# Seven block products in two more pieces of each feed-forward's first 512 gate units, and activation sums begun earlier

## The chip, the cores and the metric

The kernel runs on one core of one Trainium2 chip. The time is device microseconds (us) of one execution. The kernel before takes 2220.28 us (median of three runs, 2219.53 to 2221.06).

## The reference

A two-layer bidirectional encoder trunk in float32 on 256 tokens of width 2048. Layer 0 mixes tokens with a bidirectional mLSTM and an RG-LRU; layer 1 with 16-head dilated attention. Each layer ends in a SwiGLU feed-forward, and it is this part that the change touches:

```python
def rmsnorm(x, g):
    xf = x.astype(jnp.float32)
    y = xf * lax.rsqrt(jnp.mean(jnp.square(xf), axis=-1, keepdims=True) + RMS_EPS)
    return (y * g.astype(jnp.float32)).astype(x.dtype)

def swiglu(h, w1, w3, w2):
    return (jax.nn.silu(h @ w1) * (h @ w3)) @ w2
...
        x = x + dilated_attention(h, o_w_qkv[o], o_w_o[o]).astype(x.dtype)   # or the layer-0 mixer
        h = rmsnorm(x, f_norm[l])
        x = x + swiglu(h, f_w1[l], f_w3[l], f_w2[l]).astype(x.dtype)
```

Here `w1` (gate) and `w3` are 2048 x 5632 and `w2` is 5632 x 2048, so the hidden units form 11 blocks of 512 units, numbered 0 to 10 below.

## The kernel before

**Precision.** A float32 product is made of three products of rounded halves. Activations and weights are each split into a high part (rounded to the fp32r format) and a low part (what is left). For each weight tile ScalarE casts the high half (`wh`, L228) and VectorE subtracts to get the low half (`wl`, L229). TensorE then adds high x high, high x low and low x high in PSUM (L300 to L302 in `narrow`).

**Pieces and steps.** A weight piece is 512 input rows by 512 output columns, one transfer of 1 MB by SyncE's queue into one of three buffers (`raw`). A piece is two steps, each of 256 input rows. A plain step is 12 matmuls of 512 columns: two row blocks of 128, two token halves, three products. The list `steps` is written out in program order; `emit_step` emits one step's matmuls, and before them the split of the step three places ahead (`AHEAD`), so VectorE and ScalarE see the work of step s+3 before TensorE's step s. After each step `run_tasks` lets every waiting generator (an evacuation, a sum, an attention head) go on to its next `yield`; at most three background tasks run at once. So a task with k yields is spread over k steps, unless `until(flag)` finds its flag missing at emission: then tasks are run on at once, without steps between them.

**Seven products.** Some gate pieces (`w1`, blocks 1 to 10, pieces g = 1, 2, 3 of four) use a 2 x 2 block scheme with seven block products in place of eight (`seven_products`, L305 to L338): 21 matmuls of 256 columns a step. It needs sums of weight blocks, made once per piece (`weight_sums`, L197 to L211: four VectorE subtractions L202 to L205, then three ScalarE casts L209 and three VectorE remainders L210), and sums of activation blocks (`sf`), made once per feed-forward by the task `act_sums`: for each of six pairs of row blocks (kb = 4, 6 of piece 1; 8, 10 of piece 2; 12, 14 of piece 3) five VectorE instructions (L1067, L1071, L1072, L1074, L1075), a ScalarE cast (L1077) and a VectorE remainder (L1079), with five yields. Block 0 uses plain steps alone. The sums need `xT`, the normalised transposed activations, whose quarter g is written by the evacuation of column chunk g of the output projection ahead of the feed-forward (`norm_evac`: L414 adds the residual, ScalarE squares, TensorE transposes into `nT`, L440 and L441 write `xT`).

**Around a block.** For each block the pieces alternate, w1 piece 0, w3 piece 0, w1 piece 1, and so on: 16 steps. The gate's sum lies in two PSUM buffers `acc`, with seven products in two more (`ext`) out of the same pool of four; w3's sum lies in the pool of two (`mx`). `up1` evacuates the gate: with `ext` by one ScalarE copy (L1003) and six VectorE additions (L1004 to L1009), then the Silu (L1011); `up3` multiplies it in (L1027), which frees the two `mx` buffers for the next block's w3, and transposes to `hT` (L1040, L1041). After three blocks come the matching steps of w2.

**Buffers.** Large tiles come from eight slots of 2112 elements a partition (`slot`).

Of the kernel before, what the change touches and what calls it, by code (L numbers as in the profile page):

```python
# [9 lines left out]
F32 = mybir.dt.float32  # L10
F32R = mybir.dt.float32r
# [6 lines left out]
P = 128  # L18
# [11 lines left out]
SEVEN = (1, 2, 3)  # L30
# [38 lines left out]
def trunk_kernel(ctx: ExitStack, tc: tile.TileContext, a, out):  # L69
# [14 lines left out]
    mxp = ctx.enter_context(tc.tile_pool(name="mxp", bufs=2, space=PSUM))  # L84
    ctx.enter_context(tc.manual_schedule())

    def slot(shape, dt=F32, name="s8"):
        t = s8p.tile([P, SLOT], dt, tag="s8", name=name)
        n = int(np.prod(shape))
        v = t[:, :n]  # L90
        if len(shape) == 1:
            return v
        pat = {2: "p (a b) -> p a b", 3: "p (a b c) -> p a b c", 4: "p (a b c d) -> p a b c d"}[len(shape)]
        return v.rearrange(pat, **dict(zip("abcd"[1:], shape[1:])))
# [6 lines left out]
    def ev(name="ev"):  # L101
        return evp.tile([P, CW], F32, tag="ev", name=name)
# [50 lines left out]
    steps = []  # L153
# [17 lines left out]
    def wload(src, n):  # L171
        def load(t):
            if n < 4:
                m = 2 if n else 1
                for k in range(0, 4, m):
                    load_xT(4 * n + k, m)
                    SP.dma_start(t[:, k:k + m, :], src[:, k:k + m, :])
                return
            SP.dma_start(t, src)

        return load
# [57 lines left out]
    def add_unit(src, ch, kb0, first, last, act, seven=None):  # L239

        items.append(wload(src, len(items)))
        it = len(items) - 1
        for h in range(2):
            steps.append({
                "item": it, "half": h, "last_half": h == 1, "ch": ch, "kb": kb0 + 2 * h, "act": act,
                "first": first and h == 0, "last": last and h == 1, "wide": False, "before": None, "seven": seven,
            })
# [21 lines left out]
    urgent, queue, active = [], [], []  # L269
# [190 lines left out]
    def act_norm(gains):  # L460
        def act(kb):
            until(f"xT{gains}_{kb // 4}")
            return act_x(kb)

        return act
# [523 lines left out]
    def ffn(l, gains, nxt):  # L989
        st = {}  # L990
        act = act_norm(gains)

        def up1(c):
            def gen(ch):
                while f"rstd{gains}" not in flags:
                    yield
                es = [ev("up") for t in range(2)]
                if ch.ext:
                    (c0, c1), (e0, e1) = ch.acc, ch.ext
                    l_, r_ = slice(0, 256), slice(256, CW)  # L1000
                    x0, x1 = es
                    u2 = ev("u2")[:, l_]
                    A.copy(x0, e0)  # L1003
                    V.tensor_tensor(u2, e1[:, l_], x0[:, l_], op=ALU.add)  # L1004
                    V.tensor_tensor(x1[:, l_], e1[:, r_], u2, op=ALU.add)
                    V.tensor_tensor(x1[:, r_], x1[:, l_], x0[:, r_], op=ALU.add)
                    V.tensor_tensor(x0[:, r_], x0[:, r_], u2, op=ALU.add)
                    V.tensor_tensor(x0, c0, x0, op=ALU.add)
                    V.tensor_tensor(x1, c1, x1, op=ALU.add)  # L1009
                for t in range(2):  # L1010
                    A.activation(es[t], es[t] if ch.ext else ch.acc[t], AF.Silu, scale=cur["rstd"][:, t:t + 1])  # L1011
                ch.acc = ch.ext = None
                st["e", c] = es
                flags.add(f"up{l}_{c}")
                yield

            return gen

        def up3(c):


            def gen(ch):
                while f"up{l}_{c}" not in flags:
                    yield
                es = st.pop(("e", c))
                for t in range(2):
                    V.scalar_tensor_tensor(  # L1027
                        es[t], ch.acc[t], cur["rstd"][:, t:t + 1], es[t], op0=ALU.mult, op1=ALU.mult
                    )
                ch.acc = None  # L1030
                yield
                yield from lag()
                h = st["h", c] = slot((4, 2, S), F32R, name="hT")
                for p in range(2):
                    ps = tp("hTp")
                    for k in range(2):
                        f0 = (2 * p + k) * P
                        for t in range(2):
                            transpose(ps[:, k, t * P:(t + 1) * P], es[t][:, f0:f0 + P])
                    A.copy(h[:, 2 * p:2 * p + 2, 0, :], ps)  # L1040
                    V.tensor_tensor(  # L1041
                        h[:, 2 * p:2 * p + 2, 1, :], ps, h[:, 2 * p:2 * p + 2, 0, :].bitcast(F32), op=ALU.subtract
                    )
                    for k in range(2):
                        flags.add(f"h{l}_{4 * c + 2 * p + k}")
                    yield

            return gen

        def act_h(kb):  # L1050
            until(f"h{l}_{kb}")
            return st["h", kb // 4][:, kb % 4]

        sf = {}

        def act_sums():

            for g in SEVEN:
                while f"xT{gains}_{g}" not in flags:
                    yield  # L1060
                two = slot((2, 4, 2, P), F32R, "sf")
                for j, kb in enumerate((4 * g, 4 * g + 2)):
                    f = two[:, j]
                    v = ev("sa")
                    x = xT[:, kb:kb + 2].bitcast(F32)
                    vv = v.rearrange("p (j t) -> p j t", j=2)
                    V.tensor_tensor(vv, x[:, :, 0, :], x[:, :, 1, :], op=ALU.add)  # L1067
                    a11, a21, a12, a22 = (vv[:, j, t * P:(t + 1) * P] for j in range(2) for t in range(2))
                    w = ev("sb").rearrange("p (k t) -> p k t", k=4)
                    yield  # L1070
                    V.tensor_tensor(w[:, 0], a21, a22, op=ALU.add)  # L1071
                    V.tensor_tensor(w[:, 2], a11, a21, op=ALU.subtract)  # L1072
                    yield
                    V.tensor_tensor(w[:, 1], w[:, 0], a11, op=ALU.subtract)  # L1074
                    V.tensor_tensor(w[:, 3], a12, w[:, 1], op=ALU.subtract)  # L1075
                    yield
                    A.copy(f[:, :, 0, :], w)  # L1077
                    yield
                    V.tensor_tensor(f[:, :, 1, :], w, f[:, :, 0, :].bitcast(F32), op=ALU.subtract)  # L1079
                    sf[kb] = f  # L1080
                    flags.add(f"sf{l}_{kb}")
                    yield

        def seven(kb):
            until(f"sf{l}_{kb}")
            return sf[kb]

        at_first = len(steps)
        for hidx, (c0, c1) in enumerate(UPS):
            for c in range(c0, c1):  # L1090
                chs = Chunk(up1(c)), Chunk(up3(c))
                chs[1].small = True
                for g in range(4):
                    add_unit(a["w1"][l, c][g], chs[0], 4 * g, g == 0, g == 3, act,
                             seven if c and g in SEVEN else None)
                    add_unit(a["w3"][l, c][g], chs[1], 4 * g, g == 0, g == 3, act)
            last = hidx == len(UPS) - 1
            if last:
                ssq = const.tile([P, 2, NCD], F32, name=f"ssq{l}")
            chs = []  # L1100
            for n in range(NCD):
                if not last:
                    def evac(ch, n=n):
                        c_ = (n % 2) * CW
                        for t in range(2):
                            dst = xt[n // 2][:, t, c_:c_ + CW]
                            V.tensor_tensor(dst, ch.acc[t], dst, op=ALU.add)
                        ch.acc = None
                        yield
                else:  # L1110
                    evac = norm_evac(n, nxt, ssq, xt, last=nxt < 0)
                chs.append(Chunk(evac))
            for n, kgs in ((0, range(c0, c1 - 1)), (1, range(c0, c1 - 1)), (0, (c1 - 1,)), (1, (c1 - 1,)),
                           (2, range(c0, c1)), (3, range(c0, c1))):
                for kg in kgs:
                    add_unit(a["w2"][l, n][kg], chs[n], 4 * kg, kg == c0, kg == c1 - 1, act_h)
        steps[at_first]["before"] = lambda: queue.append(act_sums())
        return ssq


# [82 lines left out]
    act = act_norm(G_O)  # L1203
# [33 lines left out]
    n = NCD - 1  # L1237
# [104 lines left out]
```

## Time and profile before

| | |
|---|---|
| time, median of three runs | 2220.28 us (2219.53 to 2221.06) |
| the profiled execution's own time | 2219.59 us |
| its span | 2217.8 us |
| TensorE busy | 2195.3 us (99%) |
| VectorE busy | 1588.9 us (72%) |
| ScalarE busy | 1156.3 us (52%) |
| DMA | 417.53 MB, mean 188 GB/s |

The span runs from the first to the last instruction; the execution is 1.8 us longer. PE is TensorE's matmuls, PEld its weight loads, DVE VectorE, ACT ScalarE, POOL GpSimd, SP SyncE. A matmul's shown duration reaches past the start of the next one, so rates are read from the distance of starts. The first feed-forward begins at about 364 us, the second at about 1484 us.

### The profile page before, as it was taken

The page shows a single profiled execution, that of the slowest core. Times are in us where ns is not written, and L with a number is a line of the kernel's source. Part 1 is how long each engine was busy: PE and PEld are TensorE (multiplying, and loading weights), DVE is VectorE, ACT ScalarE, POOL GpSimd, SP SyncE. Part 2 cuts the span into 40 slices and gives each one's busy share as a digit, 9 for nine tenths or more (in the row PEclk, how much of TensorE's full clock was granted, in tenths as well). Part 3 has the DMA queues.
Part 4 walks back from the last instruction along what each step waited for, and adds up shares of the span by engine and source line. Part 5 has one row for each costly group of instructions (what it writes and reads, how often), then busy time and mean ns, then how long its engine had stood idle before and what let it go on. Part 6 is the DMA issues. An engine that isn't in the chain of part 4 may idle for free.

```text
span 2217.8 us, 28894 instructions
## 1 busy us (share of the span) xinstructions
PE 2195.3 (99%) x11492; PEld 1881.5 (85%) x11492; DVE 1588.9 (72%) x2160; ACT 1156.3 (52%) x1555; POOL 22.6 (1%) x37
## 2 busy tenths in 40 slices
PE   9999999999999999999999999999999999999998
PEld 7887888888888888888888888888888888888886
DVE  6877756875787688578666676567867885886686
ACT  6666555544455455445554555455544553554454
POOL 0000000000000000000000000000000000000000
PEclk9999999999999999999999999999999999999999
DMA  7444555555555555555554555455555655555653
GB/s 280 174 143 148 193 201 199 171 190 190 199 181 207 179 201 201 194 197 191 177 191 174 180 185 175 171 182 180 189 190 190 208 190 190 183 203 197 215 192 131
DMA packets 61471, 417.53 MB, mean 188 GB/s; under 512 B 7060, under 2 KB 7956, under 8 KB 12568
## 3 DMA queue, kind: packets, MB, share of 16 engines
q1 hardware_dynamic: 58616, 406.69, 52.9%
q0 software_dynamic: 2288, 8.39, 1.1%
q8 instruction: 90, 1.47, 0.2%
q10 hardware_dynamic: 432, 0.61, 0.1%
q14 instruction: 45, 0.37, 0.0%
HBM read 413.56 MB, written 2.10 MB: 187 GB/s over the span
## 4 chain that ended last, share of the span: by engine, by line
PE 90%; DVE 6%; ACT 2%; issue 1%; DMA 0%; SPq 0%; POOL 0%; POOLq 0%; DVEq 0%; ACTq 0%
PE acc L300 20%; PE acc L301 20%; PE acc L302 20%; PE acc L361 9%; PE acc L362 5%; PE ext L338 2%; PE ext L337 2%; PE ext L336 2%; DVE wl L229 2%; PE acc L338 2%; PE acc L336 2%; PE acc L337 2%; ACT wh L228 1%; PE hTp L146 1%; PE rgp L524 1%
## 5 line engine op out<-in xcount | busy, mean ns | idle before, releaser
L229 DVE TENSOR_TENSOR wl<-raw,wh 128x1024 fp32r<-128x1024 f32 (+1 forms) x770 | 928.7, 1220 | 519.9 <-ACT wh L228 517.1
L228 ACT CAST wh<-raw 128x1024 fp32r<-128x1024 f32 (+1 forms) x770 | 794.0, 1046 | 518.8 <-PE acc L302 376.2
L300 PE MATMUL acc<-wh,xT 128*128 128x512 f32 x1184 | 467.5, 395 | 0.0
L301 PE MATMUL acc<-wl,xT 128*128 128x512 f32 x1184 | 462.9, 391 | 1.0 <-DVE wl L229 1.0
L302 PE MATMUL acc<-wh,xT 128*128 128x512 f32 x1184 | 461.6, 390 | 0.0
L361 PE MATMUL acc<-xT,wh 128*128 128x512 f32 x896 | 321.7, 402 | 0.5 <-ACT v L731 0.5
L300 PE MATMUL acc<-wh,hT 128*128 128x512 f32 x704 | 276.1, 392 | 0.0
L302 PE MATMUL acc<-wh,hT 128*128 128x512 f32 x704 | 274.3, 390 | 0.0
L301 PE MATMUL acc<-wl,hT 128*128 128x512 f32 x704 | 274.1, 389 | 0.1
L302 PEld LDWEIGHTS acc<-wh,xT 128*128 128x128 f32 x1184 | 222.7, 188 | 47.2
L300 PEld LDWEIGHTS acc<-wh,xT 128*128 128x128 f32 x1184 | 223.4, 189 | 45.7 <-issue 1.5
L301 PEld LDWEIGHTS acc<-wl,xT 128*128 128x128 f32 x1184 | 223.1, 188 | 44.9 <-DVE wl L229 2.3
L362 PE MATMUL acc<-xT,wl 128*128 128x256 f32 x896 | 251.2, 280 | 0.2 <-DVE wl L229 0.2
L209 ACT CAST wf<-ws 128x512 fp32r<-128x512 f32 x180 | 111.9, 622 | 201.1 <-DVE ws L202 152.5
L361 PEld LDWEIGHTS acc<-xT,wh 128*128 128x128 f32 x896 | 168.3, 188 | 39.5 <-ACT v L731 0.6
L362 PEld LDWEIGHTS acc<-xT,wl 128*128 128x128 f32 x896 | 169.2, 189 | 1.1 <-DVE wl L229 0.5
L302 PEld LDWEIGHTS acc<-wh,hT 128*128 128x128 f32 x704 | 132.1, 188 | 27.8
L301 PEld LDWEIGHTS acc<-wl,hT 128*128 128x128 f32 x704 | 132.3, 188 | 27.4 <-DVE wl L229 0.5
L300 PEld LDWEIGHTS acc<-wh,hT 128*128 128x128 f32 x704 | 132.2, 188 | 26.8
L210 DVE TENSOR_TENSOR wf<-ws,wf 128x512 fp32r<-128x512 f32 x180 | 113.3, 684 | 0.0
L338 PE MATMUL ext<-wf,sf 128*128 128x256 f32 x240 | 68.7, 286 | 4.6 <-DVE sf L1079 4.6
L336 PE MATMUL ext<-wf,sf 128*128 128x256 f32 x240 | 68.3, 285 | 3.6 <-ACT sf L1077 3.6
(278 smaller groups left out, 2731.8 us busy)
## 6 DMA issues: line engine op xcount, KB each, us to landing
raw<-in_w SPq DMA_DIRECT2D x264, 1024.0 KB, 4.9
raw<-in_w_aqk SPq DMA_DIRECT2D x32, 1024.0 KB, 4.9
raw<-in_w_out SPq DMA_DIRECT2D x16, 1024.0 KB, 4.9
raw<-in_w_av SPq DMA_DIRECT2D x16, 1024.0 KB, 4.9
raw<-in_w_o SPq DMA_DIRECT2D x16, 1024.0 KB, 4.9
raw<-in_w_xr SPq DMA_DIRECT2D x8, 1024.0 KB, 6.8
raw<-in_w_qk SPq DMA_DIRECT2D x8, 1024.0 KB, 4.9
raw<-in_w_og SPq DMA_DIRECT2D x8, 1024.0 KB, 4.8
```

The source lines that it names most:

```text
L209: A.copy(f[:, 0], t)
L210: V.tensor_tensor(f[:, 1], t, f[:, 0].bitcast(F32), op=ALU.subtract)
L228: A.copy(hi[:, k], raw[:, k])
L229: V.tensor_tensor(lo[:, k], raw[:, k], hi[:, k].bitcast(F32), op=ALU.subtract)
L300: PE.matmul(acc, xh, hi[:, j, :], start=f, stop=False)
L301: PE.matmul(acc, xh, lo[:, j, :], start=False, stop=False)
L302: PE.matmul(acc, xl, hi[:, j, :], start=False, stop=e)
L336: PE.matmul(o, xh, wh, start=new, stop=False)
L337: PE.matmul(o, xh, wl, start=False, stop=False)
L338: PE.matmul(o, xl, wh, start=False, stop=end)
L361: PE.matmul(acc, wh[:, j, :], x2.rearrange("p a b -> p (a b)"), start=f, stop=False)
L362: PE.matmul(acc[:, :S], wl[:, j, :], x2[:, 0, :], start=False, stop=e)
```

## The change

Four edits.

1. In block 0 the gate's pieces are taken in the order 0, 3, 1, 2, and the last two of these (pieces 1 and 2) use seven products. w3's pieces keep their order. Blocks 1 to 10 stay as they are.
2. So block 0's evacuation takes the way with `ext`, and each of the two pieces gets its weight sums.
3. The task `act_sums` is put in the queue 12 steps earlier, that is 12 steps before the end of the output projection, in place of at the feed-forward's first step. It still waits for the flag of each quarter of `xT`.
4. The tile of activation sums starts 56 elements (224 bytes) into its slot.

```diff
-    def slot(shape, dt=F32, name="s8"):
+    def slot(shape, dt=F32, name="s8", off=0):
         t = s8p.tile([P, SLOT], dt, tag="s8", name=name)
         n = int(np.prod(shape))
-        v = t[:, :n]
+        v = t[:, off:off + n]
...
-                two = slot((2, 4, 2, P), F32R, "sf")
+                two = slot((2, 4, 2, P), F32R, "sf", off=56)
...
-                for g in range(4):
-                    add_unit(a["w1"][l, c][g], chs[0], 4 * g, g == 0, g == 3, act,
-                             seven if c and g in SEVEN else None)
-                    add_unit(a["w3"][l, c][g], chs[1], 4 * g, g == 0, g == 3, act)
+
+                order, at_seven = (range(4), SEVEN) if c else ((0, 3, 1, 2), (2, 3))
+                for k, g in enumerate(order):
+                    add_unit(a["w1"][l, c][g], chs[0], 4 * g, k == 0, k == 3, act,
+                             seven if k in at_seven else None)
+                    add_unit(a["w3"][l, c][k], chs[1], 4 * k, k == 0, k == 3, act)
...
-        steps[at_first]["before"] = lambda: queue.append(act_sums())
+        steps[at_first - 12]["before"] = lambda: queue.append(act_sums())
```

**Where the instructions now stand, first place.** VectorE at the end of the first output projection. L414 and L441 are the evacuation of its column chunks, L229 the splits of coming steps, L1067 to L1079 the activation sums. Before, from the splits ahead of the last chunk's evacuation on:

```order
L229 TENSOR_TENSOR wl<-raw,wh 128x1024 x5
L414 TENSOR_TENSOR xres<-acc,xres 128x512 x2
L229 TENSOR_TENSOR wl<-raw,wh 128x1024
L441 SCALAR_TENSOR_TENSOR xT<-nT,cpk,xT 128x256 x4
L448 TENSOR_REDUCE rstd_3180<-ssq_o_115 128x2
L449 TENSOR_SCALAR rstd_3180<-rstd_3180 128x2
L1067 TENSOR_TENSOR sa<-xT 128x512
L229 TENSOR_TENSOR wl<-raw,wh 128x1024
L1071 TENSOR_TENSOR sb<-sa 128x128
L1072 TENSOR_TENSOR sb<-sa 128x128
L229 TENSOR_TENSOR wl<-raw,wh 128x1024
L1074 TENSOR_TENSOR sb<-sb,sa 128x128
```

And now, from the evacuation of the second chunk on:

```order
L441 SCALAR_TENSOR_TENSOR xT<-nT,cpk,xT 128x256 x2
L229 TENSOR_TENSOR wl<-raw,wh 128x1024 x2
L1067 TENSOR_TENSOR sa<-xT 128x512
L229 TENSOR_TENSOR wl<-raw,wh 128x1024
L1071 TENSOR_TENSOR sb<-sa 128x128
L1072 TENSOR_TENSOR sb<-sa 128x128
L229 TENSOR_TENSOR wl<-raw,wh 128x1024
L1074 TENSOR_TENSOR sb<-sb,sa 128x128
L1075 TENSOR_TENSOR sb<-sa,sb 128x128
L229 TENSOR_TENSOR wl<-raw,wh 128x1024 x2
L414 TENSOR_TENSOR xres<-acc,xres 128x512 x2
L1079 TENSOR_TENSOR sf<-sb,sf 128x4x128
```

The first pair's sums now stand ahead of the third chunk's evacuation (this L414), where before they stood behind the fourth's.

**Second place.** VectorE where the last pair's sum (the sixth L1079, kb = 14) is written. L202 to L210 are weight sums of a coming gate piece. Before, in block 1, behind that block's third weight sums and ahead of its evacuation (L1004):

```order
L229 TENSOR_TENSOR wl<-raw,wh 128x1024
L1067 TENSOR_TENSOR sa<-xT 128x512
L229 TENSOR_TENSOR wl<-raw,wh 128x1024
L1071 TENSOR_TENSOR sb<-sa 128x128
L1072 TENSOR_TENSOR sb<-sa 128x128
L229 TENSOR_TENSOR wl<-raw,wh 128x1024
L1074 TENSOR_TENSOR sb<-sb,sa 128x128
L1075 TENSOR_TENSOR sb<-sa,sb 128x128
L229 TENSOR_TENSOR wl<-raw,wh 128x1024 x2
L1079 TENSOR_TENSOR sf<-sb,sf 128x4x128
L229 TENSOR_TENSOR wl<-raw,wh 128x1024
L1004 TENSOR_TENSOR u_3884<-ext,up 128x256
```

And now, right behind block 0's evacuation, around the first weight sums of block 1:

```order
L229 TENSOR_TENSOR wl<-raw,wh 128x1024
L1074 TENSOR_TENSOR sb<-sb,sa 128x128
L1075 TENSOR_TENSOR sb<-sa,sb 128x128
L229 TENSOR_TENSOR wl<-raw,wh 128x1024
L1027 SCALAR_TENSOR_TENSOR up<-acc,rstd_3205,up 128x512 x2
L202 TENSOR_TENSOR ws<-raw 128x512
L203 TENSOR_TENSOR raw<-raw 128x2x256
L204 TENSOR_TENSOR ws<-raw,ws 128x512
L205 TENSOR_TENSOR ws<-raw,ws 128x512
L210 TENSOR_TENSOR wf<-ws,wf 128x512 x3
L229 TENSOR_TENSOR wl<-raw,wh 128x1024
L1079 TENSOR_TENSOR sf<-sb,sf 128x4x128
```

The last sum has moved from behind the third to behind the first of block 1's three weight sums. In front of block 0's L1027 there now stand the six additions L1004 to L1009, four small rows of that last sum and two splits.

**Third place.** TensorE in block 0, at the ninth of its 16 steps (a piece of the difference: before with -, now with +).

```order
-L300 MATMUL acc<-wh,xT 128x512
-L301 MATMUL acc<-wl,xT 128x512
-L302 MATMUL acc<-wh,xT 128x512
+L336 MATMUL ext<-wh,xT 128x256
+L337 MATMUL ext<-wl,xT 128x256
+L338 MATMUL ext<-wh,xT 128x256
+L336 MATMUL ext<-wf,sf 128x256
+L337 MATMUL ext<-wf,sf 128x256
+L338 MATMUL ext<-wf,sf 128x256
```

Steps 9, 10, 13 and 14 of block 0 (counted from 1) change so; the transposes of the output projection's last chunk (`nT`) stand where they stood, behind block 0's first step.

## The prediction

> **What bounds the kernel now.** I read the page's busy shares first, then TensorE's list of waits, the table by stretches around the waits, the timeline there, and last the chain of waits. The page:
>
> ```profile
> PE 2195.3 (99%) x11492; PEld 1881.5 (85%) x11492; DVE 1588.9 (72%) x2160; ACT 1156.3 (52%) x1555; POOL 22.6 (1%) x37
> ...
> L338 PE MATMUL ext<-wf,sf 128*128 128x256 f32 x240 | 68.7, 286 | 4.6 <-DVE sf L1079 4.6
> L336 PE MATMUL ext<-wf,sf 128*128 128x256 f32 x240 | 68.3, 285 | 3.6 <-ACT sf L1077 3.6
> ```
>
> TensorE is busy for 99% of the span, so time comes off only by fewer matmul columns or out of the little waiting there is. Two groups hold most of that: products that wait for the activation sums `sf`. TensorE's list of waits (total, times, longest) shows one wait of each kind per feed-forward:
>
> ```profile
> PE ext L338 <- DVE sf L1079: 4.6, 2, 2.3
> PE ext L336 <- ACT sf L1077: 3.6, 2, 1.8
> PE num L796 <- ACT q L763: 1.4, 1, 1.4
> ```
>
> These 8.2 us are not the whole price. The table by stretches (length; busy time with instructions of PE, PEld, DVE, ACT, POOL; granted clock; DMA), first a stretch with the 1.4 us wait, then the two around the first waits for `sf`:
>
> ```profile
> 214.00:218.00 4.00, 2.62 (x14) 2.02 (x13) 3.67 (x9) 2.40 (x4) 0.00 (x0) 1.00 0.00 0
> ...
> 444.00:448.00 4.00, 0.50 (x2) 0.30 (x2) 3.47 (x6) 1.57 (x2) 0.00 (x0) 0.87 0.87 293
> 448.00:452.00 4.00, 3.62 (x17) 3.62 (x18) 0.32 (x1) 0.00 (x0) 0.00 (x0) 0.50 0.51 215
> ```
>
> Behind the two waits the granted clock is 0.50: the matmuls that follow run at half rate. The timeline (start, duration, idle before) gives the full loss, in both feed-forwards:
>
> ```profile
> 440.90 0.28 PE L336 MATMUL ext<-wh,xT 128*128 128x256 f32 x1
> ...
> 445.57 0.39 PE L336 MATMUL ext<-wf,sf 128*128 128x256 f32 x1 [1.80 <-ACT sf L1077]
> ...
> 448.38 0.58 PE L338 MATMUL ext<-wf,sf 128*128 128x256 f32 x1 [2.31 <-DVE sf L1079]
> ...
> 453.85 0.40 PE L300 MATMUL acc<-wh,xT 128*128 128x512 f32 x1
> ...
> 1560.79 0.28 PE L336 MATMUL ext<-wh,xT 128*128 128x256 f32 x1
> ...
> 1573.58 0.39 PE L300 MATMUL acc<-wh,xT 128*128 128x512 f32 x1
> ```
>
> From the first product of block 1's last gate piece (440.90) to 453.85 lie two steps of seven products and three plain matmuls. Undisturbed steps of both kinds:
>
> ```profile
> 402.67 0.39 PE L300 MATMUL acc<-wh,xT 128*128 128x512 f32 x1
> ...
> 405.39 0.39 PE L300 MATMUL acc<-wh,xT 128*128 128x512 f32 x1
> ...
> 432.92 0.28 PE L336 MATMUL ext<-wh,xT 128*128 128x256 f32 x1
> ...
> 435.44 0.40 PE L300 MATMUL acc<-wh,xT 128*128 128x512 f32 x1
> ```
>
> Twelve plain matmuls take 2.72 us (0.227 each), the 21 of a seven-product step 2.52 us (0.120 each). Two steps and three matmuls should take 2 x 2.52 + 3 x 0.227 = 5.72 us. They took 12.95 and 12.79 us, so the two places lose 7.2 and 7.1 us, 14.3 together: 8.2 of waiting, the other 6.1 at half rate.
>
> Why are the sums late? The chain of waits runs through VectorE and ScalarE in front of that place:
>
> ```profile
> 408.37 1.06 ACT wh L228
> 409.45 1.23 DVE wl L229
> ...
> 447.72 0.61 DVE sf L1079
> 448.38 0.58 PE ext L338
> ```
>
> From 408 us to 448 us it doesn't touch TensorE. The sums go forward by one yield a step, each behind that step's split, and block 1's three weight sums stand among them.
>
> **The change, part by part.** *The late sums.* The same twelve sets of instructions (six per feed-forward) start 12 steps, 12 x 2.72 = 33 us, sooner. In the new order the last L1079 follows the split of block 1's fifth step; TensorE needs it in the 14th. For block 0's own products the sums of kb = 4 and 6 stand ahead of the split of its second step and are needed in steps 9 and 10; those of 8 and 10 stand behind the splits of steps 6 and 11 and are needed in steps 13 and 14. A split leads its matmuls by three steps (8 us), so all come in time. What hides them in the output projection is VectorE's idle time there, about 1.5 us ahead of each split:
>
> ```profile
> 359.59 1.23 DVE L229 TENSOR_TENSOR wl<-raw,wh 128x1024 fp32r<-128x1024 f32 x1 [1.50 <-ACT wh L228]
> ...
> L1067 DVE TENSOR_TENSOR sa<-xT 128x512 f32<-128x512 f32 x12 | 8.2, 684 | 0.0
> L1075 DVE TENSOR_TENSOR sb<-sa,sb 128x128 f32<-128x128 f32 x12 | 3.5, 292 | 0.4
> L1079 DVE TENSOR_TENSOR sf<-sb,sf 128x512 fp32r<-128x512 f32 x12 | 8.2, 684 | 0.0
> ```
>
> One pair costs 0.68 + 4 x 0.29 + 0.68 = 2.5 us of VectorE over five steps, 0.5 a step. If that cover were gone, each pair would add its 2.5 us. With the waits the half rate behind them goes as well: **-14.3 us**.
>
> *Fewer columns.* Two pieces of two steps in two feed-forwards are 8 steps, each 2.72 - 2.52 = 0.20 us shorter: **-1.6 us**. (The Trainium skill, TensorE: Matmul & The Clock Gate, Back-to-back issue gap, gives N/2.4 + 2.5 ns for an isolated matmul, 216 and 109 ns here, an estimate of 0.30 us a step and 2.4 us in all. The rows give 227 and 120 ns, about 11 ns more on either, which weighs against 21 matmuls in place of 12; I keep 1.6.)
>
> *VectorE's new work in block 0.* Weight sums, splits, evacuation, and what the evacuation waits for (timeline of block 1, and ScalarE's table load in block 0):
>
> ```profile
> 412.31 0.68 DVE L202 TENSOR_TENSOR ws<-raw 128x512 f32<-128x512 f32 x1
> ...
> 416.77 1.22 DVE L229 TENSOR_TENSOR wl<-raw,wh 128x1024 fp32r<-128x1024 f32 x1
> 417.91 0.29 DVE L1074 TENSOR_TENSOR sb<-sb,sa 128x128 f32<-128x128 f32 x1
> ...
> 454.47 0.42 DVE L1004 TENSOR_TENSOR u<-ext,up 128x256 f32<-128x256 f32 x1
> ...
> 456.97 0.68 DVE L1009 TENSOR_TENSOR up<-acc,up 128x512 f32<-128x512 f32 x1
> 459.40 2.36 DVE L229 TENSOR_TENSOR wl<-raw,wh 128x1024 fp32r<-128x1024 f32 x2 [1.75 <-ACT wh L228]
> 461.68 1.40 DVE L1027 SCALAR_TENSOR_TENSOR up<-acc,rstd,up 128x512 f32<-128x512 f32 x2
> ...
> 403.99 1.28 ACT L1011 ACT_TABLE_LOAD   x1
> ```
>
> One piece's weight sums take 416.77 - 412.31 = 4.46 us, a split 417.91 - 416.77 = 1.14. From block 0's first weight sums to block 1's the new order has 12 splits (13.7 us), two weight sums (8.9), the six additions (456.97 + 0.68 - 454.47 = 3.2), two L1027 (1.4) and the rest of the activation sums (about 5): 32.2 us. TensorE's 12 steps there take 8 x 2.72 + 4 x 2.52 = 31.8 us. So VectorE is as loaded as TensorE for this stretch. It enters with the three steps' lead of 8 us and no backlog, so its own splits are in time; in block 1, with 16 splits, three weight sums and an evacuation (about 37 us against 42), it catches up. ScalarE, busy 52%, takes the six added casts. No transfer is added and no queue passed; pieces 1 to 3 come in another order. A piece's buffer is held longer through its weight sums, as in blocks 1 to 10 today, and TensorE's list of waits names no DMA.
>
> What does come late is L1027, which frees block 0's `mx` buffers for block 1's w3. TensorE reaches that w3 four plain steps, 10.9 us, after block 0's last seven products. Today in block 1 the same way takes from 452.60, where the step behind the last products begins, to the end of the first L1027, 461.68 + 0.74 = 462.4: 9.8 us. Block 0 adds the table load (1.28; in block 1 the Silu is loaded already) and two small rows of the last sum (0.5): 11.6 us. So a **new wait of 0.7 us** stands ahead of block 1's first w3 matmul, with everything behind it on TensorE, twice: **+1.4 us**. Its bounds are 0 (if the table load hides) and 2.1 us each (if one more split and a small row stand in front, 1.14 + 0.29).
>
> *The offset of 224 bytes.* TensorE loads these sums as weights, VectorE and ScalarE write them. The nearest rows are VectorE's writes at 8 bytes past an aligned start (`xr`) and at an aligned one (`gr`):
>
> ```profile
> L388 DVE TENSOR_TENSOR xr<-acc,xr 128x256 f32<-128x256 f32 x8 | 3.3, 418 | 0.0
> L388 DVE TENSOR_TENSOR gr<-acc,gr 128x256 f32<-128x256 f32 x8 | 3.3, 417 | 0.0
> ```
>
> No difference, and weights from `xT` and from slots, whose starts differ, both go at 0.120 us. I take 0. No row excludes a gain or a loss for weight loads; the last rival prices that.
>
> The sum is -14.3 - 1.6 + 1.4 = -14.5 us: 2219.6 (the profiled execution) becomes 2205.1. The median shown is 0.7 us above that execution, so **2206 us** for the median.
>
> **The rivals.** *The new wait grows and takes the clock along.* At its upper bound, 2.1 us, plus half rate for as much as now (6.1 / 2 = 3.05 us), it takes 5.2 us in each feed-forward, and 15.9 - 10.4 = 5.5 us remain: 2215. For it: VectorE has no slack there. Against it: the single 1.4 us wait left the clock at 1.00, and half rate followed only where TensorE worked 0.50 of 4 us. (The Trainium skill, same page, The HAM clock gate, has the clock halved after about one idle window of 3.4 us; the stretch of 0.50 in 4 agrees, and by that rule one wait of 2.1 us would not do it.)
>
> *The stall only moves.* Block 0 now needs sums too; if they wait for a slot or fall behind the third and fourth chunks' evacuations, TensorE stops in block 0 as it did in block 1, and only 1.6 - 1.4 remain: 2220. For it: such a wait has no trace yet. Against it: the four sums' places in the order, given above, and two of the eight slots free beside four tiles of the projection's input and two of the residual.
>
> *Slower: weight loads from the shifted sums lose time.* 12 of a seven-product step's 21 matmuls have `sf` as their weights, in 128 steps: 1536 matmuls. It decides from 14.5 / 1536 = 9.4 ns each, where the gain is gone; at 20 ns the time is 2206 + 30.7 = 2237. For it: TensorE's weight loads are busy 85% of the span, so little hides them. Against it: the equal rows above.
>
> **How the numbers follow.** The forecast gets 0.80, the grown wait 0.07, the moved stall 0.07, the slower loads 0.06. The forecast's own range is 2203.5 (no new wait gives 2204.4, less a little for spread) to 2209 (both waits at 2.1 us: 2208.6). For 8 times in 10 I add some way towards the grown wait: 2203.5 to 2211.5. Runs of this kernel tell about 0.2%, 4.4 us, from no change, that is 2215.8. Faster beyond it are the forecast and the grown wait: 0.87; the moved stall is the same: 0.07; slower 0.06.
>
> **What would show it.** Right: no L336 or L338 in TensorE's list of waits; granted clock 1.00 from 370 to 460 us; 128 steps of seven products at 0.120 us a matmul; a wait of about 0.7 us, twice, of L300 for L1027; VectorE without idle time through block 0. Wrong: a clock of 0.50 behind any wait near 400 us (grown wait), waits for `sf` near 385 us (moved stall), or a distance above 0.125 us in products with `sf` (slower loads).

## The result and the profile after

The kernel with the change takes 2201.99 us (median of four runs, 2201.32 to 2202.17), against 2219.91 us for the kernel before on the same chip (four runs, 2218.67 to 2221.06): a ratio of 0.9919, 95% interval 0.9902 to 0.9936. It is faster, as forecast, by 17.9 us; forecast were about 14, and 2202 lies below the range. The profiled execution took 2202.17 us with a span of 2200.4.

The page of the kernel after, TensorE's share, one group of products with `sf` out of the page and the other from the table of groups by shape:

```profile
PE 2182.3 (99%) x11564; PEld 1872.3 (85%) x11564; DVE 1610.3 (73%) x2200; ACT 1163.9 (53%) x1569; POOL 21.8 (1%) x37
L338 PE MATMUL ext<-wf,sf 128*128 128x256 f32 x256 | 71.8, 280 | 0.0
```

```profile
L336 PE MATMUL ext<-wf,sf 128*128 128x256 f32 x256 | 71.5, 279 | 0.0
```

The groups have grown from 240 to 256 instructions (the eight new steps), and the 4.6 and 3.6 us of waiting in front of them are gone. TensorE's list of waits now (total, times, longest):

```profile
PE acc L300 <- DVE up L1027: 2.1, 2, 1.0
PE acc L300 <- ACT wh L228: 1.4, 2, 1.2
PE num L796 <- ACT q L763: 1.4, 1, 1.4
```

The two waits for `sf` are off the list; new on it is the wait for L1027, once per feed-forward. (The 1.4 us for `wh` lie ahead of the first feed-forward.) The stretches (length; busy time with instructions of PE, PEld, DVE, ACT, POOL; granted clock; DMA) of block 0 and block 1, where the clock had fallen to 0.50:

```profile
364.00:407.00 43.00, 43.00 (x235) 37.34 (x234) 38.16 (x61) 23.86 (x33) 0.72 (x1) 1.00 0.57 195
407.00:449.50 42.50, 41.47 (x248) 36.48 (x247) 36.99 (x49) 25.78 (x32) 0.00 (x0) 1.00 0.54 194
```

TensorE is busy throughout but for the one wait of 1.0 us, and the granted clock is 1.00 in both. Two more readings come from TensorE's timeline. The new wait, with the first plain matmul behind block 0's last products ahead of it (402.73), and two seven-product steps of block 1, each from its first product (L336 of `wh`,`xT` into `ext`) to the first matmul of the next step:

```profile
402.73 0.40 PE L300 MATMUL acc<-wh,xT 128*128 128x512 f32 x1
...
413.42 0.39 PE L302 MATMUL acc<-wh,xT 128*128 128x512 f32 x1
414.83 0.47 PE L300 MATMUL acc<-wh,xT 128*128 128x512 f32 x1 [1.03 <-DVE up L1027]
...
423.81 0.28 PE L336 MATMUL ext<-wh,xT 128*128 128x256 f32 x1
...
426.27 0.40 PE L300 MATMUL acc<-wh,xT 128*128 128x512 f32 x1
...
434.25 0.28 PE L336 MATMUL ext<-wh,xT 128*128 128x256 f32 x1
...
436.73 0.40 PE L300 MATMUL acc<-wh,xT 128*128 128x512 f32 x1
```

The wait sets two matmuls 1.41 us apart where 0.23 is usual: it costs 1.2 us, not only the 1.03 listed. And the steps are **shorter than before**: 426.27 - 423.81 = 2.46 us and 436.73 - 434.25 = 2.48, where the prediction read 2.52. The median of all 128 steps is 2.473 us, against 2.520 before; the mean is 2.481, against 2.525 in the same steps without the offset (the first experiment below). Nothing in the prediction makes these matmuls faster, and 128 x 0.044 = 5.6 us are more than the 4 us by which the forecast of 2206 was too long.

### The profile page after: what moved, and what is told of

The parts are those of the page before. It is cut to its first block, busy times and chain, and to the rows that moved or that the text cites. A ratio compares the mean times of both kernels' runs of the same rounds, so it can differ in the third digit from the quotient of the medians.

```text
span 2200.4 us, 29084 instructions
## 1 busy us (share of the span) xinstructions
PE 2182.3 (99%) x11564; PEld 1872.3 (85%) x11564; DVE 1610.3 (73%) x2200; ACT 1163.9 (53%) x1569; POOL 21.8 (1%) x37
## 4 chain that ended last, share of the span: by engine, by line
PE 93%; DVE 3%; ACT 2%; issue 1%; DMA 0%; SPq 0%; POOL 0%; POOLq 0%; DVEq 0%; ACTq 0%
PE acc L300 20%; PE acc L301 20%; PE acc L302 20%; PE acc L361 9%; PE acc L362 5%; PE ext L338 3%; PE ext L337 3%; PE ext L336 3%; PE acc L337 2%; PE acc L336 2%; PE acc L338 2%; DVE wl L229 1%; ACT wh L228 1%; PE hTp L146 1%; PE rgp L524 1%
## 5 line engine op out<-in xcount | busy, mean ns | idle before, releaser
L229 DVE TENSOR_TENSOR wl<-raw,wh 128x1024 fp32r<-128x1024 f32 (+1 forms) x770 | 928.1, 1220 | 480.3 <-ACT wh L228 477.9
L300 PE MATMUL acc<-wh,xT 128*128 128x512 f32 x1152 | 454.7, 395 | 3.5 <-DVE up L1027 2.1
L301 PE MATMUL acc<-wl,xT 128*128 128x512 f32 x1152 | 449.7, 390 | 1.2 <-DVE wl L229 1.2
L302 PE MATMUL acc<-wh,xT 128*128 128x512 f32 x1152 | 448.9, 390 | 0.0
L300 PEld LDWEIGHTS acc<-wh,xT 128*128 128x128 f32 x1152 | 216.6, 188 | 48.9 <-issue 4.3
L302 PEld LDWEIGHTS acc<-wh,xT 128*128 128x128 f32 x1152 | 216.3, 188 | 46.1
L301 PEld LDWEIGHTS acc<-wl,xT 128*128 128x128 f32 x1152 | 216.7, 188 | 43.4 <-DVE wl L229 2.2
L209 ACT CAST wf<-ws 128x512 fp32r<-128x512 f32 x192 | 119.5, 623 | 213.4 <-DVE ws L202 161.6
L210 DVE TENSOR_TENSOR wf<-ws,wf 128x512 fp32r<-128x512 f32 x192 | 120.9, 685 | 0.0
L338 PE MATMUL ext<-wf,sf 128*128 128x256 f32 x256 | 71.8, 280 | 0.0
L337 PE MATMUL ext<-wf,sf 128*128 128x256 f32 x256 | 71.8, 280 | 0.0
```

Of the source, the lines that this page charges most:

```text
L209: A.copy(f[:, 0], t)
L210: V.tensor_tensor(f[:, 1], t, f[:, 0].bitcast(F32), op=ALU.subtract)
L229: V.tensor_tensor(lo[:, k], raw[:, k], hi[:, k].bitcast(F32), op=ALU.subtract)
L300: PE.matmul(acc, xh, hi[:, j, :], start=f, stop=False)
L301: PE.matmul(acc, xh, lo[:, j, :], start=False, stop=False)
L302: PE.matmul(acc, xl, hi[:, j, :], start=False, stop=e)
```

## The experiments

Times are medians; each is set against the kernel before as run in the same session (2219.6, 2219.5, 2219.3 and 2218.3 us in the four that followed the first). Beside them I use the length of each feed-forward in the profiled execution, from the last transpose (`nT`) of the output projection ahead of it to the last `nT` behind it, or for the second to the start of the last matmul. What lies ahead of the first feed-forward differs by up to 1 us between kernels that do the same there (368.2 us in the change, 367.2 in the change without the offset), so these lengths separate small effects better than the medians:

| kernel | median us | first feed-forward | second |
|---|---|---|---|
| before | 2219.91 | 729.45 | 721.53 |
| sums earlier alone (e3_early_only) | 2206.12 | 722.41 | 714.50 |
| the change without the offset (e1_off0) | 2207.14 | 722.95 | 715.17 |
| the change | 2201.99 | 720.16 | 712.39 |
| offset alone (e2_offset_only) | 2214.35 | 727.44 | 718.86 |
| the change, Silu table early (e7_silu_early) | 2198.42 | 718.58 | 711.12 |

### Each part alone

Three kernels: the change with the offset taken back, the offset alone on the kernel before, and the earlier sums alone on the kernel before.

```diff
 e1_off0 (from the change)
-                two = slot((2, 4, 2, P), F32R, "sf", off=56)
+                two = slot((2, 4, 2, P), F32R, "sf")
 e2_offset_only (from before): only that line the other way round
 e3_early_only (from before)
-        steps[at_first]["before"] = lambda: queue.append(act_sums())
+        steps[at_first - 12]["before"] = lambda: queue.append(act_sums())
```

> The changed kernel with its activation sums put back to the start of their slots; nothing else differs. Theory (the offset shortens seven-product steps): in the changed kernel's trace a step of seven products takes 2.468 us (median of 106), before 2.520; without the offset the distance of products returns to 0.120 us, a step to 2.52 us, and 128 steps x 0.05 us = 6.4 us come back: 2208.4 us. The distances with weights from xT stay as they are. Rival (the shorter distance comes from the new order of work, for instance fewer collisions with VectorE, and the offset does nothing, as I predicted): 2202.0 us, steps at 2.47 us.

> The kernel before with the offset of 56 elements alone. Theory: 120 steps of seven products shorten by 0.05 us each, 6.0 us, and both stalls for the sums stay (about 7 us each): 2213.9 us. Rival (offset does nothing): 2219.9 us. A third way: if the gain lies partly in the stalls, the waits for sf would differ from 4.6 and 3.6 us in total.

> The kernel before with the activation sums begun 12 steps earlier alone: no offset, block 0 with plain steps. Theory: both stalls go with their half rate, 14.3 us, and no wait for L1027 arises since block 0 keeps its short evacuation: 2219.9 - 14.3 = 2205.6 us. Rival (the stall moves, or part of it stays as a wait of VectorE's later work): more than 2208 us, with a wait named in TensorE's list.

Measured: e1 2207.14 us (2206.59 to 2207.6; ratio 0.9944, interval 0.9932 to 0.9957), e2 2214.35 (2213.38 to 2215.49; 0.9977, 0.9968 to 0.9987), e3 2206.12 (2205.57 to 2207.03; 0.994, 0.9928 to 0.9953). So the offset gives 5 us by medians on either kernel (4.7 and 5.6 by the feed-forwards, with 120 and 128 such steps), and without it the change lands 1 us from the forecast. The offset alone leaves both waits for `sf` as they were; TensorE's list of waits of that kernel:

```profile
PE ext L338 <- DVE sf L1079: 4.4, 2, 2.3
PE ext L336 <- ACT sf L1077: 3.7, 2, 1.8
```

The distances of matmul starts say where its gain lies: the median step of seven products is 2.520 us in before, e1 and e3, and 2.473 in after and e2. Within the step, matmuls whose stationary operand is `sf` stand 117 ns apart on the mean; from one with `xT` to the next with `sf` it is 118, from `sf` back to `xT` 114. All stood 120 apart without the offset.

### What the offset does: bursts

Three theories could explain a shorter distance between matmuls: where the stationary operand starts by itself, where the moving one starts by itself, or the distance between the two starts. A kernel without the trunk runs bursts of 48 fp32r matmuls with both operands' starts varied, first with the other engines idle, then with VectorE and ScalarE busy (e4_bench). Its output leaves out the whole computation.

```python
PE.matmul(acc[:, :n], wgt[:, ws:ws + P], mov[:, ms:ms + n], ...)   # ws = w + 128 i, ms = m + 512 j
```

> No trunk at all: bursts of 48 matmuls each (fp32r, 256 or 512 columns, weights cycling through slices of 128 columns) at chosen start offsets of the weights and of the moving operand in elements of 4 bytes, first with the other engines idle, then for a few offsets with VectorE and ScalarE streaming. The output is not the trunk's: it is left out whole. Theory A (the start of a weight load alone decides): with idle engines 256-column matmuls go at 0.120 us for weight offsets that are multiples of 64 elements and at 0.113 to 0.118 us at 56, whatever the moving offset; the same nanoseconds come off 512 columns (0.227 to about 0.220). Theory B (weights and moving operand collide when both start alike): the gain depends on the difference of the two offsets, so 56 against 56 is again 0.120 and 0 against 56 gains as much as 56 against 0. Theory C (a collision with VectorE's and ScalarE's traffic): with idle engines no offset matters, and a difference shows only in the second part.

Mean distance of starts within a burst, its first matmuls left out, in ns, worked out from the trace (starts in columns of 4 bytes; 56 is the change's; seven of 30 pairs of starts):

```
stationary, moving     256 columns   512 columns
 0,  0                    120.0         226.9
56,  0                    117.8         233.3
 0, 56                    118.2         233.3
56, 56                    119.9         226.7
64,  0                    119.9         226.7
48,  0                    117.8         228.8
16,  0                    113.3         233.3
```

With VectorE and ScalarE busy the values are the same within about 1 ns (120.0, 116.7, 118.3, 120.0 and 226.7, 233.3, 233.3, 226.9 for the first four). Both shifted does nothing, and 64 columns (256 bytes) do nothing: what counts is the **distance of the two starts within 256 bytes**, and not one start by itself. The other 23 pairs bear this out at 512 columns, where pairs of one distance agree within 1 ns. At 256 columns they do so in part only: 0, 48 lies at the same distance as 16, 0 and 8, 56, and takes 117.8 ns where those take 113.3; 0, 16 takes 113.3 where 48, 0 and 40, 56 take 117.8. So at 256 columns something besides the distance counts too, and no run here shows what. The second column was no part of any theory: with 512 columns the change's difference costs 6.4 ns.

### Other offsets in the kernel

```diff
-                two = slot((2, 4, 2, P), F32R, "sf", off=56)
+                two = slot((2, 4, 2, P), F32R, "sf", off=64)      # e6_off64; off=16 in e5_off16
```

> The changed kernel with the offset at 64 elements (256 bytes). Theory (in the bursts 64 elements gave 0.120 us again, as 0 did): steps at 2.52 us and 2207.1 us, as with no offset. Rival (any shift within the slot helps, for instance by another layout of the buffers or another order of waits): 2202.0 us.

> The changed kernel with the sums' offset at 16 elements (64 bytes) in place of 56. Theory (the distance of 256-column matmuls depends on where the weights start against the moving operand, as in the bursts: 0.120 us at equal starts, 0.118 at 56, 0.1133 at 16): the 12 matmuls of a step with sf as weights go at about 0.1133, a step takes 12 x 0.1133 + 9 x 0.120 = 2.44 us in place of 2.47, and 128 steps give 3.8 us: 2198.2 us. Rival (any start off the grid gives the same): 2202.0 us.

256 bytes: 2207.09 us (2206.58 to 2207.28; ratio 0.9945, interval 0.9932 to 0.9958), the time without any offset, as expected. 64 bytes: 2203.15 (2202.71 to 2203.64; 0.9928, 0.9915 to 0.9941), **a miss**: the 113.3 ns of the bursts would have made it 2198. One of its steps in TensorE's timeline, which took 2.48 us in after (434.25 to 436.73):

```profile
433.23 0.28 PE L336 MATMUL ext<-wh,xT 128*128 128x256 f32 x1
...
435.73 0.40 PE L300 MATMUL acc<-wh,xT 128*128 128x512 f32 x1
```

2.50 us (the median of all 128 is 2.493), so 64 bytes are worse than 224 here, where in the bursts they were better. Between matmuls with `sf` it is 117.5 ns on the mean, not 113.3, and near the 117.8 of the pair 0, 48 at the same distance. Either what surrounds the matmuls counts as well, or the bursts' mix of addresses is not the step's.

### The steps without the trunk

To tell these apart, a kernel holds nothing but the 21 matmuls of a step at the addresses that their operands have in the trunk, 12 steps for each of 17 starts of the sums, no other engine at work (e10_bench_steps).

```python
def sa(k):    # one of the sums as stationary operand; off = 0, 4, 8 ... 64
    return [at(SLOTS[g - 1] + 4 * (off + half * 1024 + k * 256 + i * P), P) for i in range(2)]
```

> No trunk: only the 21 matmuls of a seven-product step, at the addresses that their operands have in the kernel, with no other engine at work, 12 steps for each of 17 starts of the sums (0, 16, 32 ... 256 bytes later; in columns 0, 4, 8 ... 64). Its output is not the reference's: the whole computation is left out. Theory (the length of a step goes by the operands' starts alone): the steps take what they take in the kernels, 2.520 us at 0, 2.493 at 64 bytes, 2.468 to 2.475 at 224, 2.520 at 256, and so the other starts show whether one is better than 224 bytes. Rival (what surrounds the matmuls counts too, as the bursts' 113.3 ns at 64 bytes suggests): steps of other lengths than these, nearer to 2.38 (21 x 113.3 ns) at 64 bytes.

TensorE's timeline, three pairs of rows: the first matmul of the third of the 12 steps and that of the twelfth, nine steps later, at 0, at 192 and at 224 bytes:

```profile
39.68 0.28 PE L81 MATMUL acc<-big 128*128 128x256 f32 x1
...
62.36 0.28 PE L81 MATMUL acc<-big 128*128 128x256 f32 x1
...
398.96 0.28 PE L81 MATMUL acc<-big 128*128 128x256 f32 x1
...
420.92 0.28 PE L81 MATMUL acc<-big 128*128 128x256 f32 x1
...
457.96 0.28 PE L81 MATMUL acc<-big 128*128 128x256 f32 x1
...
480.22 0.28 PE L81 MATMUL acc<-big 128*128 128x256 f32 x1
```

22.68 us for nine steps are 2.520 each (0 bytes), 21.96 are 2.440 (192), 22.26 are 2.473 (224). The whole list, the mean of nine steps in us:

```
bytes    0     16    32    48    64    80    96    112   128   144   160   176   192   208   224   240   256
step   2.520 2.487 2.488 2.500 2.493 2.493 2.480 2.502 2.480 2.512 2.507 2.487 2.440 2.471 2.473 2.489 2.520
```

0, 64, 224 and 256 bytes give 2.520, 2.493, 2.473 and 2.520, the medians that the trunk's steps have. So at these four starts the sequence of addresses alone sets the distance; the bursts missed at 64 bytes because they ran through another sequence, not because the trunk disturbs. And 224 bytes are not the best of the 17 starts: 192 are.

### The same offset where the columns are 512

If the sign goes by the columns, the same 224 bytes must hurt where the stationary operand meets 512 moving columns. The down projection's hidden activations (`hT`) do (e9_hidden_offset).

```diff
-                h = st["h", c] = slot((4, 2, S), F32R, name="hT")
+                h = st["h", c] = slot((4, 2, S), F32R, name="hT", off=56)
```

> The change, with the hidden activations' slots (hT, the stationary operand of the down projection's 512-column matmuls) begun 224 bytes late as well, like those of the sums. In the bursts a 256-column matmul went from 120.0 to 117.8 ns when the stationary operand alone began 224 bytes late, but a 512-column one went from 226.9 to 233.3. Theory (what counts is the distance of the two operands' starts within 256 bytes, and its sign goes by the columns): the down projection's 704 products of three matmuls take 6.6 ns more each, 704 x 3 x 6.6 ns = 13.9 us, so 2202.0 + 13.9 = about 2216, and the matmuls of the hidden activations stand 233 ns apart. Rival (the bursts' 512 columns do not carry over to the kernel, as the 113.3 ns of 32 bytes less did not): within 3 us of 2202.

2213.51 us (2212.59 to 2214.05; ratio 0.9973, interval 0.9964 to 0.9983): 11.5 us worse than the change, 13.9 expected; the feed-forwards are 6.0 and 6.2 us longer. The groups by shape (count; busy us, mean ns), of after and of this kernel:

```profile
L302 PE MATMUL acc<-wh,hT 128*128 128x512 f32 x704 | 274.3, 390 | 0.0
```

```profile
L302 PE MATMUL acc<-wh,hT 128*128 128x512 f32 x704 | 278.0, 395 | 0.0
```

The starts of these matmuls stand 233 to 234 ns apart where they stood 227, as in the bursts; 2112 matmuls of 6 ns are 12.7 us. One edit of one kind, put on two tiles of the same kernel, gains 5 us on one and loses 11 on the other.

### The new wait: the Silu's table

In front of block 0's first L1027, ScalarE and VectorE of the kernel after:

```profile
407.53 1.28 ACT L1011 ACT_TABLE_LOAD   x1 [3.37 <-DVE up L1008]
408.82 1.34 ACT L1011 ACTIVATE up<-up,rstd 128x512 f32<-128x512 f32 x2
410.07 1.99 ACT L228 CAST wh<-raw 128x1024 fp32r<-128x1024 f32 x2
```

```profile
407.37 0.68 DVE L1009 TENSOR_TENSOR up<-acc,up 128x512 f32<-128x512 f32 x1
...
411.13 1.22 DVE L229 TENSOR_TENSOR wl<-raw,wh 128x1024 fp32r<-128x1024 f32 x1 [2.68 <-ACT wh L228]
...
413.94 1.40 DVE L1027 SCALAR_TENSOR_TENSOR up<-acc,rstd,up 128x512 f32<-128x512 f32 x2
```

The table load stands in front of the Silu, the casts of two coming splits stand behind the Silu, and VectorE sits idle for 2.68 us until the first of them is done, before it comes to L1027. The load has no input to wait for, so it can be moved: a Silu of one column ahead of the activation sums of piece 3.

```diff
                 two = slot((2, 4, 2, P), F32R, "sf", off=56)
+                if g == SEVEN[-1]:
+                    A.activation(sm(1, "pre"), ones[:, 0:1], AF.Silu)
```

> The changed kernel with one Silu of a single column ahead of the last third of the activation sums, so that ScalarE loads the Silu's table in block 0 before the evacuation needs it. Theory (the wait of L300 for L1027, 1.03 us in each feed-forward, is the length of block 0's evacuation chain, of which 1.28 us is that load): the wait goes, and 2 x 1.03 = 2.1 us with it: 2199.9 us. Rival (VectorE's load in block 0 sets the wait, the table load hides): the wait stays near 1 us and the time at 2202.0 us.

2198.42 us (2197.82 to 2199.16; ratio 0.9907, interval 0.9891 to 0.9923). ScalarE and VectorE, and the stretch of block 1, of this kernel:

```profile
386.88 1.05 ACT L228 CAST wh<-raw 128x1024 fp32r<-128x1024 f32 x1 [0.39 <-PE acc L302]
387.95 1.28 ACT L1063 ACT_TABLE_LOAD   x1
...
406.78 1.34 ACT L1011 ACTIVATE up<-up,rstd 128x512 f32<-128x512 f32 x2 [3.38 <-DVE up L1008]
```

```profile
409.09 1.23 DVE L229 TENSOR_TENSOR wl<-raw,wh 128x1024 fp32r<-128x1024 f32 x1 [1.41 <-ACT wh L228]
...
411.90 1.41 DVE L1027 SCALAR_TENSOR_TENSOR up<-acc,rstd,up 128x512 f32<-128x512 f32 x2
```

```profile
407.00:449.50 42.50, 42.50 (x253) 37.56 (x252) 38.06 (x52) 24.27 (x31) 0.00 (x0) 1.00 0.55 192
```

VectorE's 2.68 us have become 1.41, shorter by about the load's 1.28; L1027 comes in time and TensorE has no gap left in the stretch. The feed-forwards are 1.6 and 1.3 us shorter, 2.9 together, where 2.1 were expected: the two waits cost 1.2 us each in full, and the other 0.5 is not traced. (The medians differ by 3.6; this kernel's profiled execution also reached its first feed-forward 0.7 us sooner.) (The Trainium skill, ScalarE: Activation LUTs, What ACT_TABLE_LOAD costs, gives about 1283 ns for the load, which the rows show; it adds a drain of 1380 ns, and no such time shows here: in the change the Silu starts 0.01 us behind the load, and where the load was moved it starts 0.02 us behind the cast ahead of it.)

### The sums late, with block 0's new products

The earlier start and block 0's products came in one change. Without the first, the second has its sums late in block 0 as well (e8_sums_late):

```diff
-        steps[at_first - 12]["before"] = lambda: queue.append(act_sums())
+        steps[at_first]["before"] = lambda: queue.append(act_sums())
```

> The changed kernel with the activation sums begun at the feed-forward's first step again, block 0's seven products kept. Theory (the early start is what block 0's products need): with one yield a step only the first pair of sums is ready by step 9; the other three are waited for in steps 10, 13 and 14, each at about the 4.1 us of waits and 3.1 us of half rate that one late pair cost before, so 3 x 7.2 = 22 us in each feed-forward: about 2245 us, and not under 2220. Rival (the sums catch up on their own, and the early start only helps block 1): about 2202 + 14 = 2216 us with waits in block 1 alone.

2237.23 us (2237.07 to 2237.38; ratio 1.0082, interval 1.0063 to 1.0101), slower than before. Its waits, and its stretches of blocks 0 and 1:

```profile
PE ext L338 <- DVE sf L1079: 13.4, 4, 5.9
PE ext L336 <- ACT sf L1077: 10.1, 4, 3.7
```

```profile
364.00:407.00 43.00, 35.78 (x177) 30.53 (x175) 32.44 (x52) 21.66 (x30) 1.08 (x1) 0.92 0.45 159
407.00:470.00 63.00, 57.12 (x318) 49.60 (x317) 49.85 (x75) 30.34 (x39) 0.00 (x0) 0.95 0.47 163
```

Two waits of each kind per feed-forward in place of one, and the clock falls in both stretches. All of them stand in block 0, in steps 10, 13 and 14, as the first expectation has it: 5.9, 1.4 and 0.8, 3.7 us. The feed-forwards are 17.9 and 17.8 us longer than the change's, 22 expected; the rival, with waits in block 1 alone and 14 us in all, falls.

### The best of both

```diff
 (from e7_silu_early)
-                two = slot((2, 4, 2, P), F32R, "sf", off=56)
+                two = slot((2, 4, 2, P), F32R, "sf", off=48)
```

> The change, with the one-column Silu among the sums (the kernel that took 2198.4) and the sums' slot begun 192 bytes late instead of 224 (48 columns for 56). Theory (a step's length goes by the operands' starts alone): without the trunk the step of 21 matmuls took 2.440 us at 192 bytes against 2.473 at 224, so in the kernel the 128 steps of 2.468 to 2.475 come down to about 2.44, 128 x 0.03 = 3.8 us: 2198.4 - 3.8 = about 2194.6. Rival (the steps without the trunk are no measure at a start that the kernel has not had): within 1 us of 2198.4.

2195.92 us (2195.13 to 2196.2; ratio 0.9897, interval 0.988 to 0.9913), 22.4 us below the kernel before in its own session and the fastest of all. A step of block 1 in its timeline:

```profile
433.04 0.28 PE L336 MATMUL ext<-wh,xT 128*128 128x256 f32 x1
...
435.48 0.40 PE L300 MATMUL acc<-wh,xT 128*128 128x512 f32 x1
```

2.44 us, the length it had without the trunk. The gain is 2.5 us by medians and 1.4 + 1.7 = 3.1 by the feed-forwards (717.19 and 709.40), not 3.8: the expectation took typical steps, but some steps are longer, and the mean step fell by 0.024 us (128 x 0.024 = 3.1), not by 0.03.

## Why the prediction was right and wrong

**The late sums: right.** Forecast were 7.2 and 7.1 us. Alone, the earlier start shortens the feed-forwards by 729.45 - 722.41 = 7.04 and 721.53 - 714.50 = 7.03 us. That the half rate behind the waits belongs to their price is shown: the listed waits were only 8.2 us of the 14.1. The cover held, too: the stretch between the feed-forwards is 390.4 us in both kernels, with the sums inside it.

**Fewer columns and the new wait: a gain of 0.2 us forecast, a small loss measured.** Against the earlier sums alone, block 0's products cost 0.54 and 0.67 us. The wait was mis-sized: 0.7 us forecast, 1.03 listed, 1.2 in full. From 402.73 to the first L1027's end (413.94 + 0.74) are 11.9 us where 11.6 were forecast, and the matmul starts another 0.2 us later. The table load that I named belongs to it: move the load and the wait goes. With 1.2 the two terms give -1.6 + 2.4 = 0.8 of the 1.2 measured; the other 0.4 I did not trace. As the change stands, block 0's eight shorter steps don't pay for their own wait; with the load moved, which gives back 2.9 us (1.6 + 1.2 = 2.8 were missing), they do.

**The offset: the step that failed.** "I take 0. No row excludes a gain or a loss for weight loads; the last rival prices that." The offset gained 2.8 us in each feed-forward, 5.2 by medians, and this alone put the time outside the range: without it the change takes 2207.1, inside. The forecast began from "time comes off only by fewer matmul columns or out of the little waiting there is"; a third way, the same matmuls at a shorter distance, was left out there. Two more things were wrong in the step itself. The rows compared VectorE's writes, which are 0.418 and 0.417 us whatever the start, while TensorE reads the tile, and the sentence on `xT` and slots compared tiles that all start at multiples of 256 bytes, whose distances within 256 bytes are all 0. And having said that neither sign was excluded, I priced only a loss: the low end, 2203.5, was the forecast without the new wait and held no gain at all. A gain of the size from which that rival decides, 9.4 ns each or 14.4 us, would have put the low end at 2206 - 14.4 = 2191.6, and half of that near 2199.

In feed-forward lengths the whole is 14.07 (sums) - 1.21 (block 0) + 5.57 (offset) = 18.43 us, the parts put on in this order. The spans differ by 2217.8 - 2200.4 = 17.4, as the change's profiled execution reached its first feed-forward 1.0 us later.

**The rivals.** *The grown wait with the clock*: no, the granted clock is 1.00 behind a wait of 1.0 us. *The stall only moves*: no, but its mechanism is real: with the late start it costs 35 us (e8). *Slower loads from shifted sums*: the start does move the distance, about 2 ns a matmul faster over the 21 of a step here, and at 512 columns some 6 ns slower (e9); it had the right place and the wrong sign. **VectorE without idle time through block 0** was wrong as well: 38.16 us busy of 43.00, and 2.68 us of idle time right ahead of L1027. L1027 was late for ScalarE's order, in which the table load and the Silu stand ahead of the casts, and not for VectorE's own load alone.

## What to carry to other kernels

A change of a tile's start is a change of every matmul that reads it: run the real matmuls at their real addresses for a few starts before costing it at nothing, and don't expect the sign to be the same for another number of moving columns. When a row says that neither sign is excluded, the range needs both. And a table load can be moved to a place where nobody waits for what stands behind it on the engine; in front of a chain that TensorE waited for, its 1.28 us cost 1.3 to 1.6 us here.

## What the runs showed of the hardware

Two fp32r matmuls in a row, each with its own weight load, stand 120.0 ns apart at 256 columns and 226.7 to 227.4 at 512 where the stationary and the moving operand start at the same place within 256 bytes. At the other distances tried it was 113.3 to 120.0 ns at 256 columns and 228.8 to 234.4 at 512: a difference never helped the wide matmul, and helped the narrow one at most distances. VectorE and ScalarE, idle or busy, changed it by 1.1 ns at most. At 512 columns the distance alone gave the value within 1 ns; at 256 some bursts of one distance differ by 4.5 ns, and over a step of 21 matmuls the best start was another than in the bursts (2.440 us at 192 bytes, 2.512 at 144). What in the memory or in TensorE's reading makes it so stays open; no run here shows that. (The Trainium skill, SBUF — State Buffer, Operand start alignment, says where an operand may start and that its runs timed nothing; these runs put a time beside it.)

In the kernels before and after, half rate followed where waits came close together: 1.8 and 2.3 us within 4.6 us brought the clock to 0.50, single ones of 1.0 and 1.4 us left it at 1.00. With the sums late (e8), a single wait of 5.9 us brought it to 0.55 in a stretch of 4 us, and 1.4 and 0.8 us within 2.7 us left it at 1.00. Where the bound between these lies, the runs don't show.
